# First token tile in two halves, the second tile ahead of the last first weights, and six warm-up products in place of nine

## The chip, the core and the metric

The kernel runs on one core of a Trainium2 chip. The core has a matrix engine (PE, with its weight loads shown apart as PEld), a vector engine (DVE), a scalar engine (ACT), GpSimd (POOL) and a queue processor (SP) that issues most transfers. PE multiplies a stationary block of 128 x 128 with a moving block of up to 512 columns and adds into one of eight banks of PSUM. The metric is the device time in microseconds of one execution; lower is better.

## The reference

One residual block over 512 tokens of width 1024 in float32: an input projection of the normalised tokens feeds a pooling mixer and a gated recurrence (a causal convolution, gates and a scan over the tokens), both merged by gates; then a gated feed-forward part with a convolution, and a gated embedding.

```python
h = rms_norm(x, g_mix_pre[l])
z = h @ w_in[l]                       # 1024 x 4608: pool 512, recurrence 1024, its gate 1024, gates 2048
u_pool, u_rx, u_rg = z[..., :c0], z[..., c0:c1], z[..., c1:c2]
y_pool = pool_mixer(u_pool, pool_w[l], pool_scale[l]) @ w_pool_out[l]
y_rnn = rg_lru_branch(u_rx, u_rg, ...) @ w_rg_out[l]
x = x + rms_norm((gate_pool * y_pool + gate_rnn * y_rnn) @ w_o[l], g_mix_post[l])
...                                   # feed-forward: w_up, causal convolution, gelu, w_down
x = x + ple_gate * ple
```

The part that matters here is the very first: the first 512 columns of `u_rx`, the projection that the recurrence needs first.

## The kernel before

Products are made in float32 precision from parts: each operand is a high part (a cast, on ACT) and a low part (value minus high part, on DVE), and a product is high x high + low x high + high x low. `quad("A")` holds the tokens' high and low parts (tiles A in the profile); `hi` and `lo` are those of a weight block, `raw` the block as fetched.

Tokens come transposed: `x_t[k]` is tile k, 128 channels by all 512 tokens, fetched into `xraw[k]` (tiles m in the profile). There are eight. For each, ACT multiplies by the norm's gain `gmix` into the high part (L556) and DVE makes the low part (L557). `gmix` is a small transfer of its own on ACT's queue (L229). The row scale of the norm is applied later, to the results.

The weights for the first four output tiles, `w_rx`, come in four blocks of two channel tiles each (`("rx", 0)` to `("rx", 3)`). The first block is fetched and cast in three pieces, columns 0 to 256, 256 to 512 and 512 to 1024 (`FIRST`, L464 to 474); the first two serve channel tile 0, the third serves tile 1. The stage's products (L580 to 586) go over the eight channel tiles; for each, 4 output tiles x 3 parts, 512 columns each, into four banks: 96 products.

Before that, `WARM` products of a 128 x 128 block of ones run on PE (L240, L241; in float32 each shows as two passes). Nothing reads their result.

After the 96 products come the tiles of the rest of `w_in` (`in_tile`, L641). Inside the first of them, after three channel tiles, `spread_rstd` (L633 to 638) runs four small products of `ones` with four diagonals (tiles t in the profile), which spread the tokens' row scales over all partitions. DVE makes the diagonals at L591 from the scales.

PE's order is that of the code. On the other engines a scheduler orders the instructions from the order of the code, their dependencies and a few explicit ones (`behind`). SP issues its transfers in order, and each waits for the landing of the eighth one before it among these queues. The line that makes the diagonals:

```python
behind(V.tensor_scalar(diag[:, t * P : (t + 1) * P], ident, rstd1[:, t : t + 1], None, ALU.mult), low_of["in", 0])
```

Of the kernel before, what the change touches and what calls it, by code (L numbers as in the profile page):

```python
# [53 lines left out]

PLACES, PLACE_UP, PLACE_H2 = 64, 48, (1072, 46)
URGENT = 700
WARM = 9

FIRST = (0, 256), (256, 512), (512, 1024)
IN_ORDER = [("gate", _g) for _g in range(4)]  # L60
# [23 lines left out]
def block_kernel(  # L84
# [361 lines left out]
    def prep(key):  # L446
        if key[0] == "up" and key not in parts:
            up_form(*key[1:])
            return
        if key in parts:  # L450
            hi, lo = parts_of(D)
            for i, v in enumerate((hi, lo)):
                nc.sync.dma_start(v.bitcast(F32), parts[key][i])
            if key[0] == "up":
                hi, lo = (v.rearrange("p (j c) -> p j c", j=2) for v in (hi, lo))
            ready[key] = (hi, lo)
            return
        ap = src[key]
        n = 1
        for d in ap.shape[1:]:  # L460
            n *= d
        raw = wpool.tile([P, n], F32, tag="raw", name=nm("raw"), bufs=6)
        dst = raw if len(ap.shape) == 2 else raw.rearrange("p (k c) -> p k c", k=ap.shape[1])
        if key == order[0]:  # L464
            nc.sync.dma_start(xraw[0], x_t[0])
            for a, b in FIRST:
                nc.sync.dma_start(raw[:, a:b], ap.rearrange("p k c -> p (k c)")[:, a:b])
        else:
            nc.sync.dma_start(dst, ap)
        hi, lo = parts_of(n)  # L470
        if key == order[0]:
            for a, b in FIRST:
                ACT.copy(hi[:, a:b], raw[:, a:b])
                sub(lo[:, a:b], raw[:, a:b], hi[:, a:b].bitcast(F32))
        else:
            ins = ACT.copy(hi, raw)  # L476
# [68 lines left out]
        )  # L545
        xtok.append(xt)

    for k in range(KD):
        raw = xraw[k]
        if k == 0:  # L550
            weight(("rx", 0), ahead=0)
        else:
            nc.sync.dma_start(raw, x_t[k])
        hi, lo = ht(k)
        g = gmix[:, k : k + 1]
        ht_done.append(ACT.activation(hi, raw, AF.Identity, scale=g).ins.name)  # L556
        V.scalar_tensor_tensor(lo, raw, g, hi.bitcast(F32), ALU.mult, ALU.subtract)  # L557
        if k == 3:
# [21 lines left out]
    for k in range(KD):  # L580
        w = weight(("rx", k // 2), ahead=3)
        (wh, wl), (hh, hl) = w, ht(k)
        for i, (a, b) in enumerate(((wh, hh), (wl, hh), (wh, hl))):
            for m in range(4):
                o = (k % 2) * S + m * P
                PE.matmul(rx[m], a[:, o : o + P], turns(b), start=k == 0 and i == 0, stop=k == KD - 1 and i == 2)  # L586


    diag = temp()
# [939 lines left out]
```

## Time and profile before

| what | us |
|---|---|
| runs | 703.17, 703.72, 703.90 |
| median | 703.72 |
| the profiled execution | 702.84 |
| its span, first to last instruction | 701.1 |

The profile is of one execution. It has the busy time of each engine, the chain of work that ended last, groups of like instructions, the timeline of each engine and the transfers with the time from issue to landing. Times count from the span's start. PE's lengths overlap, since one product starts before the last has ended; how often they start is read from the start times, or from a group of n as (length of the group - length of one) / (n - 1). DVE is busy for 591.6 us of the span, ACT for 454.2, and the 16 DMA engines move 251 GB/s on the mean.

### The profile page before, as it was taken

The page shows a single profiled execution, that of the slowest core. Times are in us where ns is not written, and L with a number is a line of the kernel's source. Part 1 is how long each engine was busy: PE and PEld are TensorE (multiplying, and loading weights), DVE is VectorE, ACT ScalarE, POOL GpSimd, SP SyncE. Part 2 cuts the span into 40 slices and gives each one's busy share as a digit, 9 for nine tenths or more (in the row PEclk, how much of TensorE's full clock was granted, in tenths as well). Part 3 has the DMA queues.
Part 4 walks back from the last instruction along what each step waited for, and adds up shares of the span by engine and source line. Part 5 has one row for each costly group of instructions (what it writes and reads, how often), then busy time and mean ns, then how long its engine had stood idle before and what let it go on. Part 6 is the DMA issues. An engine that isn't in the chain of part 4 may idle for free.

```text
span 701.1 us, 11599 instructions
## 1 busy us (share of the span) xinstructions
PE 693.4 (99%) x4423; PEld 638.2 (91%) x4423; DVE 591.6 (84%) x772; ACT 454.2 (65%) x693; POOL 97.5 (14%) x123
## 2 busy tenths in 40 slices
PE   9999999999999999999999999999999999999997
PEld 8888888888889998889999999999999888888886
DVE  5698645999759998897999999999999988989972
ACT  6757789934438574488966667766667747665631
POOL 0311331322000000112011211111210210001100
PEclk9999999999999999999999999999999999999999
DMA  8999899999898897865396886896699799967111
GB/s 323 410 304 282 237 245 225 258 264 290 252 334 286 302 385 251 326 214 180 118 328 206 196 264 211 206 261 238 169 219 386 238 300 328 346 207 260 56 61 61
DMA packets 67288, 175.71 MB, mean 251 GB/s; under 512 B 6049, under 2 KB 6689, under 8 KB 66849
## 3 DMA queue, kind: packets, MB, share of 16 engines
q1 hardware_dynamic: 49808, 124.64, 49.3%
q0 software_dynamic: 17280, 50.34, 30.6%
q8 instruction: 35, 0.57, 0.3%
q14 instruction: 21, 0.16, 0.1%
q10 hardware_dynamic: 144, 0.00, 0.0%
HBM read 162.37 MB, written 62.91 MB: 321 GB/s over the span
## 4 chain that ended last, share of the span: by engine, by line
PE 89%; DVE 5%; ACT 1%; issue 1%; POOL 1%; DMA 1%; SPq 0%; ACTq 0%; DVEq 0%; POOLq 0%
PE ps L222 28%; PE ps L224 28%; PE ps L223 28%; PE ps L586 3%; POOL s L507 1%; DVE lo L191 1%; PE ps L695 1%; DMA raw<-in_w_rx_dram 1%; DVE C L191 1%; DVE m L1017 1%; PE ps L1028 0%; DMA x2d<-m 0%; DVE m L1091 0%; DVE m L1222 0%; ACT rb L512 0%
## 5 line engine op out<-in xcount | busy, mean ns | idle before, releaser
L191 DVE TENSOR_TENSOR lo<-raw,hi 128x1024 fp32r<-128x1024 f32 (+2 forms) x199 | 230.3, 1183 | 47.0 <-ACT hi L476 30.3
L222 PE MATMUL ps<-A,hi 128*128 128x256 f32 (+1 forms) x672 | 212.0, 316 | 0.5 <-ACT ps L1216 0.5
L224 PE MATMUL ps<-A,lo 128*128 128x256 f32 (+1 forms) x672 | 211.4, 315 | 0.0
L223 PE MATMUL ps<-A,hi 128*128 128x256 f32 (+1 forms) x672 | 211.4, 315 | 0.0
L476 ACT CAST hi<-raw 128x1024 fp32r<-128x1024 f32 (+1 forms) x118 | 118.2, 1013 | 58.8 <-PE ps L224 19.5
L222 PEld LDWEIGHTS ps<-A,hi 128*128 128x128 f32 x672 | 128.2, 191 | 8.8 <-issue 1.0
L224 PEld LDWEIGHTS ps<-A,lo 128*128 128x128 f32 x672 | 128.3, 191 | 6.9
L223 PEld LDWEIGHTS ps<-A,hi 128*128 128x128 f32 x672 | 128.2, 191 | 6.7
L224 PE MATMUL ps<-C,lo 128*128 128x256 f32 x376 | 103.3, 275 | 1.3 <-DVE lo L191 1.3
L222 PE MATMUL ps<-C,hi 128*128 128x256 f32 x376 | 103.7, 276 | 0.1
L223 PE MATMUL ps<-C,hi 128*128 128x256 f32 x376 | 103.3, 275 | 0.0
L195 ACT CAST hi<-raw 128x1024 fp32r<-128x1024 f32 x76 | 78.6, 1051 | 20.2 <-PE ps L223 13.1
L222 PE MATMUL ps<-hi,A 128*128 128x512 f32 x224 | 85.2, 380 | 0.0
L224 PE MATMUL ps<-hi,A 128*128 128x512 f32 x224 | 85.0, 379 | 0.0
L223 PE MATMUL ps<-lo,A 128*128 128x512 f32 x224 | 84.9, 379 | 0.0
L224 PEld LDWEIGHTS ps<-C,lo 128*128 128x128 f32 x376 | 71.8, 191 | 1.5 <-DVE lo L191 1.5
L222 PEld LDWEIGHTS ps<-C,hi 128*128 128x128 f32 x376 | 71.8, 191 | 0.6 <-ACT ps L1161 0.4
L223 PEld LDWEIGHTS ps<-C,hi 128*128 128x128 f32 x376 | 71.8, 191 | 0.3
L507 POOL TENSOR_TENSOR s<-s,mhalf 128x1 f32<-128x1 f32 (+1 forms) x21 | 17.6, 840 | 265.6 <-DVE s L523 243.8
L307 POOL DMA_DIRECT2D wdsum<-in_w_down_dram x36 | 33.2, 1056 | 141.2 <-ACT t L1157 63.5
L224 PEld LDWEIGHTS ps<-hi,A 128*128 128x128 f32 x224 | 42.3, 189 | 6.3 <-DVE A L191 0.4
L222 PEld LDWEIGHTS ps<-hi,A 128*128 128x128 f32 x224 | 42.3, 189 | 6.0
(206 smaller groups left out, 1070.9 us busy)
## 6 DMA issues: line engine op xcount, KB each, us to landing
raw<-in_w_up_dram SPq DMA_DIRECT2D x46, 512.0 KB, 5.4
wdsum<-in_w_down_dram POOLq DMA_DIRECT2D x36, 512.0 KB, 7.7
raw<-in_w_in_dram SPq DMA_DIRECT2D x32, 512.0 KB, 8.7
raw<-wdsum SPq DMA_DIRECT2D x24, 512.0 KB, 7.8
raw<-in_w_down_dram SPq DMA_DIRECT2D x18, 512.0 KB, 6.9
wosum<-in_w_o_dram POOLq DMA_DIRECT2D x12, 512.0 KB, 9.4
wdsum<-wdsum POOLq DMA_DIRECT2D x12, 512.0 KB, 5.9
raw<-wosum SPq DMA_DIRECT2D x8, 512.0 KB, 6.2
```

The lines of the kernel that those rows point to most:

```text
L191: return V.tensor_tensor(o, a, b, ALU.subtract)
L195: last_copy[0] = ACT.copy(hi, src)
L222: PE.matmul(o, ah, bh, start=start, stop=False, **kw)
L223: PE.matmul(o, ah, bl, start=False, stop=False, **kw)
L224: PE.matmul(o, al, bh, start=False, stop=stop, **kw)
L307: ins = nc.gpsimd.dma_start(o, i, **kw)
L476: ins = ACT.copy(hi, raw)
L507: last_pow[0] = nc.gpsimd.tensor_tensor(y, v, mhalf[:, :n], ALU.pow).ins.name
L586: PE.matmul(rx[m], a[:, o : o + P], turns(b), start=k == 0 and i == 0, stop=k == KD - 1 and i == 2)
L695: PE.matmul(ps, bd[pr, a, o], turns(b[pr]), start=i == 0, stop=i == 2)
L1017: ins = V.scalar_tensor_tensor(res[h], og[h], r, res[h], ALU.mult, ALU.add)
```

## The change

Three edits, all at the start.

The first token tile is fetched in two halves. A half (`quarters_of`) is two stretches of 128 tokens, 256 apart, since the products read the tokens in an interleaved order. Transfers, high parts and low parts of the halves alternate with the first two weight pieces. The second token tile is fetched and split ahead of the third weight piece. The products of channel tile 0 are made in the order of arrival: for two output tiles and half the tokens at a time, 256 columns each, 24 products in place of 12. The six of one such part need only one weight piece and one half of the tokens. `WARM` is 6.

```diff
-WARM = 9
+WARM = 6
...
         if key == order[0]:
-            nc.sync.dma_start(xraw[0], x_t[0])
-            for a, b in FIRST:
+            for j, (a, b) in enumerate(FIRST):
+                if j < 2:
+                    nc.sync.dma_start(quarters_of(xraw[0], j), quarters_of(x_t[0], j))
+                else:
+                    nc.sync.dma_start(xraw[1], x_t[1])
                 nc.sync.dma_start(raw[:, a:b], ap.rearrange("p k c -> p (k c)")[:, a:b])
...
         if key == order[0]:
-            for a, b in FIRST:
+            for j, (a, b) in enumerate(FIRST):
+                first_tokens(j)
                 ACT.copy(hi[:, a:b], raw[:, a:b])
                 sub(lo[:, a:b], raw[:, a:b], hi[:, a:b].bitcast(F32))
...
+    def quarters_of(v, j):
+        return v.rearrange("p (a b) -> p a b", a=2)[:, :, j * P : (j + 1) * P]
+
+    def tokens(k, j=None):
+        hi, lo, raw = (v if j is None else quarters_of(v, j) for v in (*ht(k), xraw[k]))
         g = gmix[:, k : k + 1]
         ht_done.append(ACT.activation(hi, raw, AF.Identity, scale=g).ins.name)
         V.scalar_tensor_tensor(lo, raw, g, hi.bitcast(F32), ALU.mult, ALU.subtract)
+
+    def first_tokens(n):
+        if n < 2:
+            tokens(0, n)
+        else:
+            tokens(1)
...
         (wh, wl), (hh, hl) = w, ht(k)
+        for q, h in ((0, 0), (0, 1), (1, 0), (1, 1)) if k == 0 else ():
+            for i, (a, b) in enumerate(((wh, hh), (wh, hl), (wl, hh))):
+                for m in (2 * q, 2 * q + 1):
+                    PE.matmul(rx[m][:, h * HALF : (h + 1) * HALF], a[:, m * P : (m + 1) * P], turns(b)[:, h * P : (h + 1) * P, :], start=(h, i) == (0, 0), stop=i == 2, skip_group_check=True)
+        if k == 0:
+            continue
         for i, (a, b) in enumerate(((wh, hh), (wl, hh), (wh, hl))):
             for m in range(4):
                 o = (k % 2) * S + m * P
-                PE.matmul(rx[m], a[:, o : o + P], turns(b), start=k == 0 and i == 0, stop=k == KD - 1 and i == 2)
+                PE.matmul(rx[m], a[:, o : o + P], turns(b), start=False, stop=i == 2, skip_group_check=True)
```

Where the instructions stand. On SP, from the program's start, before (m is a token tile, raw a weight block):

```order
L465 DMA m_139<-in_x_t_dram 128x512
L467 DMA raw_147<-in_w_rx_dram 128x256 x2
L467 DMA raw_147<-in_w_rx_dram 128x512
L553 DMA m_140<-in_x_t_dram 128x512
L469 DMA raw_165<-in_w_rx_dram 128x1024
```

and after:

```order
L467 DMA m_136<-in_x_t_dram 128x2x128
L470 DMA raw_144<-in_w_rx_dram 128x256
L467 DMA m_136<-in_x_t_dram 128x2x128
L470 DMA raw_144<-in_w_rx_dram 128x256
L469 DMA m_137<-in_x_t_dram 128x512
L470 DMA raw_144<-in_w_rx_dram 128x512
L472 DMA raw_165<-in_w_rx_dram 128x1024
```

One transfer more stands ahead of the second weight block, and the second token tile has gone ahead of the third weight piece. On ACT, the same place, before:

```order
L556 ACTIVATE A_135<-m_139,gmix 128x512
L473 CAST hi_152<-raw_147 128x256 x2
L473 CAST hi_152<-raw_147 128x512
L556 ACTIVATE A_135<-m_140,gmix 128x512
L476 CAST hi_167<-raw_165 128x1024
```

and after:

```order
L558 ACTIVATE A_132<-m_136,gmix 128x2x128
L477 CAST hi_151<-raw_144 128x256
L558 ACTIVATE A_132<-m_136,gmix 128x2x128
L477 CAST hi_151<-raw_144 128x256
L558 ACTIVATE A_132<-m_137,gmix 128x512
L477 CAST hi_151<-raw_144 128x512
L480 CAST hi_167<-raw_165 128x1024
```

The two halves alternate with the weight pieces, and the second tile's tokens precede the third piece. DVE's low parts stand in the same order. On PE, after the warm-up products, the first six products after the change (ps_263 and ps_264 are the banks of the first two output tiles, A_132 and A_134 the high and low tokens):

```order
L602 MATMUL ps_263<-A_132,hi_151 128x256
L602 MATMUL ps_264<-A_132,hi_151 128x256
L602 MATMUL ps_263<-A_134,hi_151 128x256
L602 MATMUL ps_264<-A_134,hi_151 128x256
L602 MATMUL ps_263<-A_132,lo_152 128x256
L602 MATMUL ps_264<-A_132,lo_152 128x256
```

Before, these were products of 512 columns over all four banks, with the low weights ahead of the low tokens. From the second channel tile on, PE, ACT, DVE, POOL and SP issue the same instructions in the same order before and after.

More of the change, by code (lines that the diff above doesn't have):

```diff
@@ L546, in load_tokens @@
         xtok.append(xt)
[L548 to L554, printed above, removed]
+    def quarters_of(v, j):
+        return v.rearrange("p (a b) -> p a b", a=2)[:, :, j * P : (j + 1) * P]
+    def tokens(k, j=None):
+        hi, lo, raw = (v if j is None else quarters_of(v, j) for v in (*ht(k), xraw[k]))
         g = gmix[:, k : k + 1]
@@ L557, in block_kernel @@
         V.scalar_tensor_tensor(lo, raw, g, hi.bitcast(F32), ALU.mult, ALU.subtract)
+    def first_tokens(n):
[3 more added lines that the diff above has]
+            tokens(1)
+    for k in range(KD):
+        if k == 0:
+            weight(("rx", 0), ahead=0)
+            ht_done.pop(0)
+        elif k > 1:
+            nc.sync.dma_start(xraw[k], x_t[k])
+            tokens(k)
         if k == 3:
```

1 line of the change is left out of this document (added).

## The prediction

> **What bounds the kernel now.** I read the busy times first, then the chain that ended last, then each engine's timeline of the first 30 us, since everything the change touches lies there.
>
> ```profile
> PE 693.4 (99%) x4423; PEld 638.2 (91%) x4423; DVE 591.6 (84%) x772; ACT 454.2 (65%) x693; POOL 97.5 (14%) x123
> ...
> 1.66 3.77 DMA raw<-in_w_rx_dram
> ...
> 5.90 20.56 PE ps L586 x94
> ...
> 349.63 0.11 PE ps L223
> ```
>
> PE is busy for 693.4 of 701.1 us. The chain (start, duration, what) begins with a fetch of the first weights and then stays on the 94 first products, L586. A microsecond won on PE at the start reaches the end only if no other engine holds PE up later. The last row prices a product of 256 columns: 0.11 us. These are the first rows of PE, then ACT, DVE and SP (start, duration, line, out<-in, in brackets the idle time before and what ended it):
>
> ```profile
> 1.06 4.21 PE L241 MATMUL ps<-m 128*128 128x128 f32 x18 [1.06 <-DVE mhalf L235]
> 4.92 0.80 PE L586 MATMUL ps<-A,hi 128*128 128x512 f32 x2
> 5.90 0.70 PE L586 MATMUL ps<-A,hi 128*128 128x512 f32 x2 [0.17 <-ACT hi L473]
> 6.44 1.03 PE L586 MATMUL ps<-A,lo 128*128 128x512 f32 x4
> 7.30 1.89 PE L586 MATMUL ps<-A,hi 128*128 128x512 f32 x8
> ...
> 3.64 0.72 ACT L556 ACTIVATE A<-m,gmix 128x512 fp32r<-128x512 f32 x1 [0.97 <-DMA gmix<-in_cols_dram]
> 4.27 0.39 ACT L473 CAST hi<-raw 128x256 fp32r<-128x256 f32 x1
> 5.45 0.40 ACT L473 CAST hi<-raw 128x256 fp32r<-128x256 f32 x1 [0.79 <-DMA raw<-in_w_rx_dram]
> 6.28 0.62 ACT L473 CAST hi<-raw 128x512 fp32r<-128x512 f32 x1 [0.43 <-DMA raw<-in_w_rx_dram]
> 6.96 0.73 ACT L556 ACTIVATE A<-m,gmix 128x512 fp32r<-128x512 f32 x1
> 9.54 0.72 ACT L556 ACTIVATE A<-m,gmix 128x512 fp32r<-128x512 f32 x1
> ...
> 5.06 0.42 DVE L191 TENSOR_TENSOR lo<-raw,hi 128x256 fp32r<-128x256 f32 x1
> 6.93 0.69 DVE L191 TENSOR_TENSOR lo<-raw,hi 128x512 fp32r<-128x512 f32 x1 [0.62 <-ACT hi L473]
> 7.72 0.75 DVE L557 SCALAR_TENSOR_TENSOR A<-m,gmix,A 128x512 fp32r<-128x512 f32 x1
> ...
> 0.75 0.39 SPq L465 DMA_DIRECT2D m<-in_x_t_dram  x1
> 1.19 1.37 SPq L467 DMA_DIRECT2D raw<-in_w_rx_dram  x3
> 2.60 0.43 SPq L553 DMA_DIRECT2D m<-in_x_t_dram  x1
> 11.50 0.33 SPq L469 DMA_DIRECT2D raw<-in_w_in_dram  x1
> ```
>
> Nine warm-up products, two passes each, fill PE to 4.92. The eight products from 7.30 start (1.89 - 0.38) / 7 = 0.216 us apart, 0.38 being the length of the last; the two from 4.92 start 0.80 - 0.38 = 0.42 apart, so PE still ran at half speed there. (The granted-clock column reads 1.00 throughout; I go by spacing.) After two products PE has nothing to do until the second weight quarter is cast: 4.92 + 0.80 = 5.72 to 5.90. The second token tile's products start at 7.30 + 4 x 0.216 = 8.17.
>
> **The bound that decides.** At 28 us PE runs four small products (L637) that spread the row scales. Each needs a 128-column diagonal from DVE. Rows of ACT, DVE, PE and its weight loads:
>
> ```profile
> 23.42 1.04 ACT L476 CAST hi<-raw 128x1024 fp32r<-128x1024 f32 x1 [0.64 <-DMA raw<-in_w_in_dram]
> 24.69 1.04 ACT L476 CAST hi<-raw 128x1024 fp32r<-128x1024 f32 x1 [0.23 <-DMA raw<-in_w_in_dram]
> ...
> 24.49 2.50 DVE L191 TENSOR_TENSOR lo<-raw,hi 128x1024 fp32r<-128x1024 f32 x2 [1.51 <-ACT hi L476]
> 26.91 0.67 DVE L591 TENSOR_SCALAR t<-ident,s 128x128 f32<-128x128 f32 x3
> 27.50 1.22 DVE L191 TENSOR_TENSOR lo<-raw,hi 128x1024 fp32r<-128x1024 f32 x1
> 28.63 0.28 DVE L591 TENSOR_SCALAR t<-ident,s 128x128 f32<-128x128 f32 x1
> ...
> 28.24 0.83 PE L637 MATMUL ps<-t,m 128*128 128x128 f32 x6
> 28.97 0.30 PEld L637 LDWEIGHTS ps<-t,m 128*128 128x128 f32 x2
> 29.21 0.46 PE L222 MATMUL ps<-A,hi 128*128 128x512 f32 x1
> ```
>
> Six of the eight passes start (0.83 - 0.27) / 5 = 0.11 apart, the last at 28.79; the seventh is due at 28.90 and starts at 28.97, after the fourth diagonal (28.63 + 0.28 = 28.91). PE already waits 0.07 us here. That diagonal stands on DVE behind a train without a gap from 24.49 on, which began when ACT had cast the weights that landed at 23.4. It depends on when w_in lands, not on how far PE is.
>
> **What paces the landings.** Two views: the DMA issues (KB each, us from issue to landing) and the stretches (last two columns: DMA share, GB/s).
>
> ```profile
> gmix<-in_cols_dram ACTq DMA_DIRECT2D x1, 4.0 KB, 2.9
> m<-in_x_t_dram SPq DMA_DIRECT2D x1, 256.0 KB, 2.7
> raw<-in_w_rx_dram SPq DMA_DIRECT2D x1, 128.0 KB, 3.8
> m<-in_x_t_dram SPq DMA_DIRECT2D x1, 256.0 KB, 4.3
> raw<-in_w_in_dram SPq DMA_DIRECT2D x1, 512.0 KB, 11.9
> ...
> 3.00:4.00 1.00, 1.00 (x7) 1.00 (x6) 0.00 (x0) 0.36 (x1) 0.00 (x0) 1.00 0.80 150
> 4.00:5.00 1.00, 1.00 (x7) 1.00 (x6) 0.61 (x1) 0.65 (x2) 0.00 (x0) 1.00 0.71 187
> 5.00:6.00 1.00, 0.83 (x5) 0.42 (x3) 0.60 (x3) 0.40 (x1) 0.00 (x0) 1.00 0.99 380
> 10.00:15.00 5.00, 5.00 (x25) 4.38 (x24) 4.64 (x6) 4.04 (x6) 0.00 (x0) 1.00 1.03 410
> ```
>
> From 5 us on the queues are full at 380 to 410 GB/s; the w_in tile issued at 11.50 lands 11.9 later. Its landing moves only by what the first 5 us deliver, and the change sends the same bytes.
>
> **The change, step by step.** SP issues one transfer more: tokens a, weights a, tokens b, weights b, tile 1, weights c. At 0.43 us an issue (row at 2.60) everything behind leaves up to 0.43 later. I cost this at nothing, because the queue hides it: tile 1, issued at 2.60, took 4.3 us to land at 6.9. If that cover is missing, w_in is late by up to 0.43. At their places in the bytes, weights b should land as now (1.66 + 3.77 = 5.43 in the chain), tile 1 where weights c land now (6.28 at the latest), and weights c where tile 1 lands now, 6.9.
>
> ACT: its first operation waits for gmix (0.74 + 2.9 = 3.64), not for the tokens (0.75 + 2.7 = 3.45). Half the columns cost about the 0.39 of the 256-column cast, so hi of tokens a is ready at 4.03, of weights a at 4.42. [...]
>
> Warm-ups: 18 passes start (4.21 - 0.42) / 17 = 0.22 apart, so 12 end at 1.06 + 11 x 0.22 + 0.42 = 3.9. PE idles for about 0.5 us and starts at 4.45, not 4.92: 0.47 earlier. Bounds: 3.9 if gmix comes sooner in a lighter queue, 4.92 if the first cast is no earlier.
>
> PE's first tile: 24 products of 0.11 = 2.64 us where 12 x 0.216 = 2.59 stood, 0.05 more. The twelve of weights a take 4.45 to about 6.2, the first four at half speed (0.213 each, to 5.3), with DVE's low parts (0.42 to 0.43 each, back to back from 4.05) in time for them. Weights b are cast at 5.45 + 0.40 = 5.85, so the 0.18 us hole goes. The other twelve end at 6.2 + 12 x 0.11 = 7.5.
>
> Tile 1: ACT from 6.28 to 7.0, then the cast of weights c, 0.62, ready at 7.6. PE starts tile 1 there instead of at 8.17: 0.55 earlier. DVE does 0.75 + 0.69 from 7.0 to 8.45, due at 7.6 + 0.86. Tile 2 would follow at 7.6 + 12 x 0.216 = 10.2, but its tokens are ready at 9.54 + 0.72 = 10.26. Now it starts at 8.17 + 12 x 0.216 = 10.76, so the lead is 10.76 - 10.3 = 0.46.
>
> The small products: PE arrives at 28.24 - 0.46 = 27.78, does six passes by 28.4, and waits for the fourth diagonal until 28.97, as now. L222 follows at 29.21, as now. The whole lead of 0.46 becomes a wait of 0.5. After that both programs issue the same instructions in the same order on every engine.
>
> Sum: 0.46 won, 0.46 waited, 0.0 on the span of 701.1. The profiled execution took 702.84 with 1.74 around the span; the median of the runs shown is 703.72, 0.88 above. On the runs I predict 703.7. Within 0.2% (1.4 us) is what a measurement of this kernel cannot tell from no change.
>
> **Rivals.**
> - *The lead is kept.* From 3 to 5 us only 150 and 187 GB/s moved, (2 x 390 - 337) / 390 = 1.1 us of full rate lost. If other shapes at the start remove part of that dip, rx and w_in land sooner, the diagonals with them, and PE keeps its lead. Against it: the queue was not empty in the dip and no row says what ended it. Worth 0.2 to 0.95 (PE's first tile ends at 7.5, or at 7.2 if it can start at 3.9, against 8.17 now): 702.8 to 703.5, say 703.1. It alone does not reach 0.2%.
> - *The landings slip.* The extra issue and smaller pieces (512 bytes a row) delay w_in by 0.2 to 0.6: about 704.1.
> - *Slower, because PE's clock comes late.* Now PE works without a break from 1.06 and reaches full speed after the slow pair, between 5.34 and 6.44. The change leaves a hole between 3.9 and 4.45. If the count begins anew there, 5.34 - 1.06 = 4.3 us of work from 4.45 end at 8.75: 20 slow half products by then, four fast, tile 1 at 9.2 instead of 8.17, 1.03 - 0.07 = 0.95 slower, 704.6. It decides (over 1.4 slower) if full speed comes after about 10 us: 24 x 0.213 = 5.1 puts tile 1 at 9.6, which is already 1.4 late. Against it: unbroken work is all that the trace shows before full speed, so no row tells what a hole does. [...]
>
> **Numbers.** No change, the lead lost at the diagonals: 0.42 (703.3 to 704.1 by itself). Lead kept: 0.24, of it 0.09 beyond 0.2% if small waits fall well besides. Landings slip: 0.10, of it 0.02 beyond. Clock late: 0.24, of it 0.15 beyond, since a count that a hole breaks may also begin later than at 4.45. Faster 0.09, same 0.74, slower 0.17. Range 702.7 to 705.1: down to the kept lead, up to the point from which the clock decides.
>
> **What would show it.** Right: PE's first half product near 4.45, tile 1 near 7.6, a new wait of about 0.5 before the last two passes of the small products, L222 near 29.2, w_in's first cast at 23.4. Wrong: that cast moved by more than 0.3 (either landing rival), or products of 256 columns 0.21 apart past 6 us (the clock). A change behind 30 us would mean that I missed a coupling.

## The result, and the profile after

The changed kernel took 704.51 us (median of 14 runs, 703.51 to 709.36), the kernel before 702.99 beside it; the ratio is 1.0024, 95% interval 1.0013 to 1.0035. A second comparison gave 1.0028 [1.0015, 1.0041]. It is slower by about 1.7 us. The forecast was no change. The profiled execution took 707.39 (span 705.5), 2.9 above the median of its kernel, so its waits are larger than those of most executions; a second profiled one took 707.39 as well.

SP's first issues after the change (start, duration, line, out<-in):

```profile
0.75 0.67 SPq L467 DMA_DIRECT2D m<-in_x_t_dram  x1
1.47 0.58 SPq L470 DMA_DIRECT2D raw<-in_w_rx_dram  x1
2.10 0.57 SPq L467 DMA_DIRECT2D m<-in_x_t_dram  x1
2.71 0.59 SPq L470 DMA_DIRECT2D raw<-in_w_rx_dram  x1
3.35 0.43 SPq L469 DMA_DIRECT2D m<-in_x_t_dram  x1
3.82 0.43 SPq L470 DMA_DIRECT2D raw<-in_w_rx_dram  x1
4.30 0.43 SPq L472 DMA_DIRECT2D raw<-in_w_rx_dram  x1
```

The two half fetches take 0.67 and 0.57 us to issue, and the weight pieces behind them 0.58 and 0.59, where an issue took 0.39 to 0.46 before. The second weight block leaves at 4.30, before at 3.07. The stretches of one microsecond (last two columns: DMA share, GB/s) show that the queue did not hide this. Before, the first of them (the next one stands in the prediction):

```profile
2.00:3.00 1.00, 1.00 (x7) 1.00 (x6) 0.00 (x0) 0.65 (x2) 0.00 (x0) 1.00 0.96 330
```

and after:

```profile
2.00:3.00 1.00, 1.00 (x7) 1.00 (x6) 0.00 (x0) 0.63 (x2) 0.00 (x0) 1.00 0.57 171
3.00:4.00 1.00, 0.99 (x5) 0.69 (x4) 0.07 (x1) 0.51 (x1) 0.00 (x0) 1.00 0.65 189
```

The DMA engines were busy for 57% and 65% of these two stretches, before for 96% and 80%: the transfers waited for their issue. PE and ACT after, and from the chain of waits the second weight block's fetch:

```profile
4.46 1.22 PE L602 MATMUL ps<-A,hi 128*128 128x256 f32 x4 [0.47 <-ACT hi L477]
5.90 1.06 PE L602 MATMUL ps<-A,hi 128*128 128x256 f32 x4
7.12 0.61 PE L602 MATMUL ps<-A,hi 128*128 128x256 f32 x4
8.46 1.03 PE L608 MATMUL ps<-A,hi 128*128 128x512 f32 x4
11.83 1.13 PE L608 MATMUL ps<-A,hi 128*128 128x512 f32 x4 [0.61 <-ACT A L558]
29.42 1.05 PE L659 MATMUL ps<-t,m 128*128 128x128 f32 x8
30.23 0.46 PE L222 MATMUL ps<-A,hi 128*128 128x512 f32 x1
...
6.21 0.72 ACT L558 ACTIVATE A<-m,gmix 128x512 fp32r<-128x512 f32 x1 [0.39 <-DMA m<-in_x_t_dram]
10.11 1.05 ACT L480 CAST hi<-raw 128x1024 fp32r<-128x1024 f32 x1 [2.40 <-DMA raw<-in_w_rx_dram]
24.58 2.93 ACT L480 CAST hi<-raw 128x1024 fp32r<-128x1024 f32 x3
...
4.30 5.79 DMA raw<-in_w_rx_dram
```

The second weight block lands at 10.1 instead of 8.57; ACT casts it ahead of the third tile's tokens, so PE idles 0.61 us and starts that tile at 11.83 (before 10.76). The first tile's products of 256 columns start (1.06 - 0.42) / 3 = 0.21 apart at 5.90 and 0.11 apart at 7.12: full speed came at about 7. PE reaches the small products at 29.42, 1.2 later than before, and no longer waits there; L222 follows at 30.23 instead of 29.21.

So 1.0 us is gone by 30 us in this execution. The rest goes later. Here is how much later than in the profile of before the same product starts (products counted from the end, where the order is the same in all kernels; the column heads are the start before):

| profiled execution | at 90 us | 197 | 232 | 311 | last | 
|---|---|---|---|---|---|
| changed | 1.02 | 1.02 | 3.13 | 4.51 | 4.47 |
| changed, second profile | 1.49 | 1.49 | 2.65 | 4.11 | 4.57 |

Nothing happens between 30 and 197 us, then three waits come. PE's waits from 200 to 300 us after (us in total, times, longest; the same view of before is empty), rows of ACT and POOL behind them, and the stores among the DMA issues (last number: us from issue to landing):

```profile
PE ps L224 <- DVE A L191: 1.1, 1, 1.1
PE ps L222 <- ACT hi L480: 0.7, 1, 0.7
PE ps L224 <- DVE lo L191: 0.6, 1, 0.6
...
191.58 1.05 ACT L480 CAST hi<-raw 128x1024 fp32r<-128x1024 f32 x1 [5.68 <-DMA parts<-hi]
...
181.02 1.05 POOL L307 DMA_DIRECT2D up2sum<-in_w_up_dram  x1 [4.02 <-DMA up2sum<-up2sum]
...
parts<-hi SPq DMA_DIRECT2D x2, 512.0 KB, 8.0
```

The rows of ACT, POOL and the stores before:

```profile
188.97 1.04 ACT L476 CAST hi<-raw 128x1024 fp32r<-128x1024 f32 x1 [4.09 <-issue]
...
177.25 1.05 POOL L307 DMA_DIRECT2D up2sum<-in_w_up_dram  x1 [1.78 <-DMA up2sum<-up2sum]
...
parts<-hi SPq DMA_DIRECT2D x2, 512.0 KB, 6.4
```

From 183 us on, split weights are stored to memory (`parts`), and ACT reuses the tiles when a store has landed. POOL's chain of weight sums in memory (`sum_in_dram`, each step waiting for the landing of an earlier one) ends at about that time: its last sum is issued 3.8 us later than before, the stores take 8.0 us instead of 6.4, and ACT's cast comes 2.6 us later. That train of store, cast and fetch runs from 186 to 226 us and hands its lateness to PE at 211, 225 and 275. This is read from one profile; the runs without the last two sums test it.

### The profile page after: what moved, and what is told of

Same layout as the page of the kernel before. It is cut to its first block, busy times and chain, and to the rows that moved or that the text cites. A ratio compares the mean times of both kernels' runs of the same rounds, so it can differ in the third digit from the quotient of the medians.

```text
span 705.5 us, 11615 instructions
## 1 busy us (share of the span) xinstructions
PE 694.5 (98%) x4429; PEld 638.5 (91%) x4429; DVE 592.0 (84%) x773; ACT 454.3 (64%) x694; POOL 97.0 (14%) x123
## 4 chain that ended last, share of the span: by engine, by line
PE 64%; DVE 15%; DMA 10%; ACT 7%; issue 3%; POOL 1%; SPq 1%; ACTq 0%; DVEq 0%; POOLq 0%
PE ps L222 20%; PE ps L224 20%; PE ps L223 20%; DMA parts<-hi 3%; DVE lo L191 3%; PE ps L608 2%; ACT m L166 2%; DVE m L746 1%; DMA lo<-parts 1%; ACT hi L480 1%; ACT t L166 1%; ACT hi L195 1%; POOL s L511 1%; DMA m<-in_x_dram 1%; DMA raw<-rg0sum 1%
## 5 line engine op out<-in xcount | busy, mean ns | idle before, releaser
L222 PE MATMUL ps<-A,hi 128*128 128x256 f32 (+1 forms) x672 | 212.1, 316 | 0.5 <-ACT ps L1238 0.5
L222 PEld LDWEIGHTS ps<-A,hi 128*128 128x128 f32 x672 | 128.2, 191 | 8.9 <-issue 1.0
L222 PE MATMUL ps<-C,hi 128*128 128x256 f32 x376 | 103.7, 276 | 0.1
L222 PE MATMUL ps<-hi,A 128*128 128x512 f32 x224 | 85.2, 380 | 0.0
L222 PEld LDWEIGHTS ps<-C,hi 128*128 128x128 f32 x376 | 71.8, 191 | 0.6 <-ACT ps L1183 0.3
L224 PEld LDWEIGHTS ps<-hi,A 128*128 128x128 f32 x224 | 42.3, 189 | 7.5 <-DVE A L191 1.5
L223 PEld LDWEIGHTS ps<-lo,A 128*128 128x128 f32 x224 | 42.4, 189 | 5.9
```

The costliest lines, as they stand in the source:

```text
L222: PE.matmul(o, ah, bh, start=start, stop=False, **kw)
L223: PE.matmul(o, ah, bl, start=False, stop=False, **kw)
L224: PE.matmul(o, al, bh, start=False, stop=stop, **kw)
```

## The experiments

Each kernel was compared with the kernel before on the same chip. The first four were written for two theories: A, late issues on SP; B, the late clock. Later, P is A narrowed to the pieces of 512 bytes, C is one transfer more however it is cut, and S is POOL's sums.

| run | ratio to before | medians apart, us | at 90 us | 197 | 232 | 311 | last |
|---|---|---|---|---|---|---|---|
| nine warm-ups | 1.0022 [1.0009, 1.0036] | 1.61 | 0.66 | 0.66 | 1.22 | 0.99 | 1.26 |
| six warm-ups alone | 1.0005 [0.9994, 1.0017] | 1.02 | -0.20 | -0.20 | -0.20 | -0.43 | 0.87 |
| split fetch alone | 1.0016 [1.0004, 1.0027] | 1.57 | 3.36 | 3.36 | 4.20 | 4.20 | 5.17 |
| whole fetch | 1.0005 [0.9991, 1.0018] | 0.57 | 1.72 | 1.72 | 1.72 | 1.64 | 1.87 |
| rows of 1024 bytes | 1.0002 [0.9986, 1.0018] | 1.01 | 0.32 | 0.32 | 0.32 | 0.09 | 0.18 |
| the same again | 1.0007 [0.9996, 1.0018] | 0.29 | 0.40 | 0.40 | 0.42 | 0.19 | 0.28 |
| one more issue | 0.9994 [0.9979, 1.0008] | -0.64 | -0.21 | -0.21 | -0.21 | -0.42 | -0.14 |
| pieces alone | 1.0009 [0.9992, 1.0025] | 0.16 | 2.43 | 2.44 | 2.44 | 2.21 | 2.37 |
| whole fetch, nine | 1.0008 [0.9993, 1.0022] | 0.53 | 0.94 | 0.94 | 1.59 | 2.66 | 3.31 |
| second tile ahead alone | 1.0007 [0.9998, 1.0015] | 0.65 | 0.60 | 0.60 | 1.41 | 1.18 | 1.21 |
| diagonals in one row | 1.0039 [1.0026, 1.0052] | 3.12 | -0.04 | -0.04 | 3.82 | 3.60 | 3.73 |
| changed, fewer sums | 0.9999 [0.9982, 1.0016] | 0.94 | 0.80 | 0.80 | 0.80 | 0.57 | 0.79 |
| before, more sums | 1.0003 [0.9984, 1.0022] | 0.21 | 0.62 | 0.62 | 0.62 | 0.40 | 1.21 |
| diagonals, fewer sums | 0.9983 [0.9966, 0.9999] | -0.51 | 0.14 | 0.15 | 0.15 | -0.08 | 0.12 |
| before, fewer sums | 0.9981 [0.9964, 0.9998] | -0.68 | 0.05 | 0.05 | 0.05 | -0.18 | -0.01 |
| before, sums later | 1.0034 [1.0021, 1.0047] | 2.49 | 0.72 | 0.72 | 0.72 | 3.12 | 3.21 |
| diagonals, sums later | 1.0028 [1.0016, 1.0040] | 2.07 | 0.24 | 0.24 | 0.24 | 2.70 | 2.86 |

The lateness columns are of one profiled execution each, as above; the ratio and the medians are of all runs. The two do not always say the same: the medians lie up to 1.02 us apart where the interval of the ratio still holds 1, and such a difference is neither shown nor excluded.

**Nine warm-ups in the changed kernel.**

```diff
-WARM = 6
+WARM = 9
```

> The changed kernel with nine warm-up products again, all else of the change kept. Theory A (issue): SP spends 0.57 to 0.67 us on each of the four small transfers, the second weight block leaves at 4.30 instead of 3.07 and lands at 10.1, and tile 2's products start at 11.8 instead of 10.8; warm-ups don't touch that, so tile 2 starts within 0.2 of 11.8 and the time stays about 1.5 us over the kernel before (ratio about 1.002). Theory B (clock): the hole in PE from 3.9 to 4.46 put off full speed from 5.2 to 7.05; without the hole full speed comes by 5.5 and about 1 us comes back (ratio 1.000 to 1.001).

The loss stays, 1.0022. In the profile full speed came at 4.2 us (the 18 warm-up passes took 3.75 us, before 4.21), tile 1's products had no late clock ahead of them, and the second weight block still left at 4.31. It landed at 9.2 and the third tile started at 10.9, not at 10.1 and 11.8 as A had it, so in this execution the late issue cost less. The hole after six warm-ups is not what makes the change slow.

**Six warm-ups alone, in the kernel before.**

```diff
-WARM = 9
+WARM = 6
```

> The kernel before with six warm-up products, nothing else changed. Theory A (issue): no change, ratio 0.9995 to 1.0005; tile 2 is at most 0.3 us later than 10.76, since the second weight block lands at 8.6 as before. Theory B (clock): the hole before the first product puts off full speed to 7 or later; the first tile's twelve products take 1 us longer, tile 2 starts at 11.3 or later, ratio about 1.001 to 1.002.

1.0005, by its interval not told from no change. The medians lie 1.02 us apart (0.41 to 1.37 by drawing the runs anew), so a cost of the missing warm-ups is not excluded. The profile shows none at the start: PE idled from 4.0 to 4.7 and again before 5.9, and the two products at 4.73 ran at full speed all the same (0.70 us together, like the two at 5.86). This hole did not put the clock off.

**The split fetch alone, in the kernel before.**

```diff
-            nc.sync.dma_start(xraw[0], x_t[0])
-            for a, b in FIRST:
+            for j, (a, b) in enumerate(FIRST):
+                if j < 2:
+                    halves = [v.rearrange("p (a b) -> p a b", a=2)[:, :, j * P : (j + 1) * P] for v in (xraw[0], x_t[0])]
+                    nc.sync.dma_start(*halves)
```

> The kernel before with only the first tile's fetch split in two halves of 512-byte pieces, alternating with the weight pieces; products whole, nine warm-ups, second tile's fetch behind the third weight piece as before. Theory A (issue): the second weight block leaves SP at 4.0 or later and lands at 9.5 or later, tile 2 starts at 11.3 or later, about 1 us slower than before (ratio about 1.0015). Theory B (clock): PE has no hole, so no change of the time (ratio within 0.0005 of 1).

1.0016. The issues are as slow as in the changed kernel (0.68, 0.58 and 0.56 us), and the second weight block leaves at 4.32. The scheduler also put a weight cast ahead of the first tokens on ACT, so the run holds a little more than the fetch.

**The whole fetch in the changed kernel.**

```diff
-                if j < 2:
-                    nc.sync.dma_start(quarters_of(xraw[0], j), quarters_of(x_t[0], j))
-                else:
-                    nc.sync.dma_start(xraw[1], x_t[1])
+                if j != 1:
+                    nc.sync.dma_start(xraw[j // 2], x_t[j // 2])
```

> The changed kernel with the first tile fetched in one transfer again; its parts, its products in halves, the second tile ahead of the third weight piece and six warm-ups stay. Theory A (issue): SP's issues go back to 0.4 us, the second weight block leaves at about 3.1 and lands at 8.6, tile 2 starts at 10.3 to 10.8, and the time is that of the kernel before or up to 0.4 less (ratio 0.9995 to 1.000). Theory B (clock): the hole stays (its first product is ready at about 4.7), full speed comes at 7 or later, and the time stays about 1 us over the kernel before (ratio 1.001 to 1.002).

1.0005, though the profiled execution had the late clock as the prediction's rival described it:

```profile
5.06 1.22 PE L600 MATMUL ps<-A,hi 128*128 128x256 f32 x4 [1.07 <-ACT hi L475]
8.64 0.63 PE L600 MATMUL ps<-A,lo 128*128 128x256 f32 x2
9.83 0.39 PE L600 MATMUL ps<-A,lo 128*128 128x256 f32 x2
10.05 1.03 PE L606 MATMUL ps<-A,hi 128*128 128x512 f32 x4
```

A hole of 1.07 us, products at half speed until 9.7, the second tile at 10.05; this execution ends 1.9 us later. Of the eleven executions four lie at 703.0 to 703.3 and five at 704.4 or more, the profiled 704.72 among them, so some may pay that and some not; only the profiled one shows its clock. A is borne out by the ratio, and B is not excluded as a cost in some executions.

**Rows of 1024 bytes.** The host lays the first tile half after half, so that a half is one run of 1024 bytes a row.

```diff
-                    nc.sync.dma_start(quarters_of(xraw[0], j), quarters_of(x_t[0], j))
+                    nc.sync.dma_start(xraw[0][:, j * HALF : (j + 1) * HALF], x_t[0][:, j * HALF : (j + 1) * HALF])
```

> The changed kernel, with the first token tile laid half after half in memory, so that each half is one run of 1024 bytes a row in place of two runs of 512. Seven issues on SP up to the second weight block as in the changed kernel, same bytes, same order. Theory P (the pieces of 512 bytes make the issues slow, and the slow issues make everything behind late): each early issue takes 0.39 to 0.45 us instead of 0.57 to 0.67, the second weight block leaves at 3.4 to 3.6 instead of 4.30 and lands by 9.3, the second token tile's products start at 10.3 to 11.0, the ratio to the kernel before is 0.999 to 1.001. Theory C (one transfer more is what costs, however it is cut): the ratio stays at 1.002 and PE waits 0.5 us or more at 224 to 227 us. With six warm-ups the clock may still come late: full speed at 5 to 7 us.

SP's issues in this run:

```profile
0.75 0.38 SPq L467 DMA_DIRECT2D m<-in_x_t_dram  x1
1.19 0.42 SPq L470 DMA_DIRECT2D raw<-in_w_rx_dram  x1
1.66 0.42 SPq L467 DMA_DIRECT2D m<-in_x_t_dram  x1
3.55 0.43 SPq L472 DMA_DIRECT2D raw<-in_w_rx_dram  x1
```

The same seven transfers with the same bytes: the issues are as short as before, and the second weight block leaves at 3.55, 0.48 later than before. From 2 to 4 us the DMA engines are busy for 82% and 94% of the time. The ratio falls to 1.0002, though the medians are still 1.01 us apart. At the small products PE waits as the prediction drew it:

```profile
28.21 0.83 PE L661 MATMUL ps<-t,m 128*128 128x128 f32 x6
29.29 0.49 PE L661 MATMUL ps<-t,m 128*128 128x128 f32 x2 [0.25 <-DVE t L615]
```

Six passes, then a wait for the fourth diagonal: the seventh was due at 28.87 (28.21 + 6 x 0.11) and starts at 29.29, 0.42 later. But PE comes there at 28.21, only 0.03 earlier than before; it waits because the diagonal is ready at 29.23 (before 28.91).

The edit changes two things at once: a row is one run and not two, and the runs are longer than 512 bytes. No run here separates them.

**One more issue in the kernel before.**

```diff
+        if k == 1:
+            nc.sync.dma_start(spare, cols[:, C_GMIX : C_GMIX + KD])
```

> The kernel before, with one more transfer on SP's queue behind the second token tile: 4 KB of the small columns into a tile that nothing reads. Nothing else moves. This is the step that I had costed at nothing with a bound of 0.43 us, alone. Theory P: the issue costs 0.43, the second weight block leaves at 3.5 instead of 3.07; PE's second token tile at 10.7 to 11.2; ratio 0.9995 to 1.0007, no wait of 0.4 us or more at 224 to 227. Theory C: ratio 1.001 to 1.003, and the wait at 224 to 227 appears.

The second weight block leaves at 3.55, as with rows of 1024 bytes, and the kernel is not slower (0.9994). C falls: one issue of 0.43 us costs nothing here, as I had said.

**The pieces alone, in the kernel before.** The first tile's rows lie in four pieces of 512 bytes with 16 bytes between them; one transfer.

```diff
-            nc.sync.dma_start(xraw[0], x_t[0])
+            nc.sync.dma_start(*(v.rearrange("p (a c) -> p a c", a=4)[:, :, :P] for v in (xraw[0], x_t[0])))
```

> The kernel before, with the first token tile fetched in one transfer as before, but from rows that lie in four pieces of 512 bytes with 16 bytes between them. Number and order of transfers as before. Theory P: this issue takes 0.6 to 1.4 us in place of 0.39, those behind it are slower too (0.55 or more in place of 0.42), the second weight block leaves 0.8 to 1.5 later than 3.07, and the ratio is 1.0005 to 1.002. Theory C: 0.999 to 1.0005, no matter how slow the issues are.

```profile
0.75 0.67 SPq L465 DMA_DIRECT2D m<-in_x_t_dram  x1
1.47 1.55 SPq L467 DMA_DIRECT2D raw<-in_w_rx_dram  x3
3.54 0.43 SPq L469 DMA_DIRECT2D raw<-in_w_rx_dram  x1
```

The issue itself is slow (0.67), but the three behind it take 1.55 together, hardly more than 1.37 before, and the second weight block is only 0.47 late. The ratio, 1.0009, is not told from none. P had expected 0.8 to 1.5: one such transfer is not shown to be a loss. The split fetch, which has two of them with other issues between, showed one.

**The whole fetch with nine warm-ups.** On top of the edit of the whole fetch:

```diff
-WARM = 6
+WARM = 9
```

> The changed kernel with the first token tile fetched in one transfer and with nine warm-ups: left of the change are the products by halves and the second token tile ahead of the last first weights. If the hole after six warm-ups was what put PE's full speed off to 9.72 in the run with the whole fetch and six, full speed comes at 4 to 5.5 here, the second token tile's products at 10.3 to 10.9 instead of 12.64, and the ratio falls from 1.0005 to 0.999 to 1.0000. If the rest of the start carries the loss there, the ratio stays at 1.0005 or above. Theory P has no loss here (no pieces of 512 bytes).

1.0008. Full speed came at 7.0 us even with nine warm-ups and no hole, where 4 to 5.5 was expected, so the run gives no price of the hole. The profile has the waits at 225 and 275 as well: they are not the split fetch's alone.

**The changed kernel and the rows of 1024 bytes again, side by side.**

> The changed kernel as it is, beside the runs that follow. The lost time at the start should come again: the second weight block issued at 4.3 and landed past 9, PE at L222 0.7 to 1.3 us later than 29.21, ratio 1.0015 to 1.003. The waits of 0.9 to 1.4 us near 211, 225 and 275 us decide between two readings: if the change brings them, two or three of them come again; if they are chance landings in a stretch that hangs on stores and fetches (190 to 225 us), this profile shows others, or at most one.

> The changed kernel with the first tile's halves as single rows of 1024 bytes, a second time, on the same chip as the changed kernel. Theory P (the 512-byte pieces of the two half fetches make the early issues slow, that is most of the loss): 0.9995 to 1.0008, and below the changed kernel by 0.1% or more. Theory C (something else in the change): no difference to the changed kernel.

1.0028 and 1.0007. The medians differ by 1.34 us; drawing the runs anew gives 0.62 to 2.72. In this comparison, side by side, that one edit of the layout takes back most of the loss. Waits of PE near 211, 225 and 275 us came again in the changed kernel (by the start times 0.6, 0.6 and 1.2 us lost), and not with the rows of 1024 bytes. In this profile full speed came at 9.9 us and tile 1 at 9.76, where the other one had 7.0 and 8.46. Its second weight block left at 4.31 and yet landed at 8.66, hardly later than before. So the same kernel lost 1.5 us at the start to the clock in one execution, and in the other 1.0 us, where the landing at 10.1 held PE up.

Over all profiles, the block landed at 8.66 to 11.14 in the five where it left at 4.3, and at 8.44 to 9.44 in the five whose first transfers are those of before. That the layout carries the loss is shown; that it does so through this landing in every execution is not.

**The second tile ahead, alone, in the kernel before.**

```diff
+                if j == 2:
+                    nc.sync.dma_start(xraw[1], x_t[1])
```

> The kernel before, with one part of the change alone: the second token tile is fetched and split ahead of the last first weights. Whole first tile, whole products, nine warm-ups. Predicted for this part: the last weights land at 6.9 in place of 6.3 and are cast at about 7.6, PE's products with them wait or not by that; the second tile's products start no later than 10.8. Theory P: 0.9995 to 1.0005. If this part carries a loss of its own, 1.0008 or more, with PE waiting 0.3 us or more between 6 and 9 us for weights c.

1.0007 [0.9998, 1.0015]: at most a small loss. The cast of weights c stood at 7.54 and PE waited 0.95 us for the second weight piece, cast at 6.21. That piece left at 1.66 as before and landed at 6.19; whether the transfer moved up behind it did that is not shown. With the first transfers of before it landed at 5.4 to 5.9.

**The diagonals in one row.** Rows of 1024 bytes, and DVE makes all four diagonals behind the first low parts.

```diff
-    for t in range(NT):
-        behind(V.tensor_scalar(diag[:, t * P : (t + 1) * P], ident, rstd1[:, t : t + 1], None, ALU.mult), low_of["in", 0])
+    with tc.high_priority(offset=URGENT):
+        for t in range(NT):
+            behind(V.tensor_scalar(diag[:, t * P : (t + 1) * P], ident, rstd1[:, t : t + 1], None, ALU.mult), low_of["in", 0])
```

> The changed kernel with rows of 1024 bytes as above, and the four diagonals for the small products in one row on DVE behind the low parts of the first input weights, instead of three, then other low parts, then the fourth. In the profile with rows of 1024 bytes PE waited 0.52 us for the fourth diagonal at 28.76. If that diagonal is what takes PE's lead, as predicted, the wait falls below 0.1, L222 starts at 28.9 to 29.1 instead of 29.53, and the time is 0.3 to 0.5 us lower than with the rows of 1024 bytes alone: 0.9990 to 1.0003. If another wait follows within the first 40 us, as long as the first, the time does not move.

The small products no longer wait (eight passes from 28.36) and L222 starts at 29.17 instead of 29.53: the diagonal was the bound at 29 us. The expected time was missed: with five executions, the kernel is the slowest of all, 1.0039. The lateness is -0.04 us until 197 and 3.82 at 232:

```profile
191.87 1.04 ACT L480 CAST hi<-raw 128x1024 fp32r<-128x1024 f32 x1 [7.00 <-DMA parts<-hi]
...
211.97 0.48 PE L222 MATMUL ps<-m,hi 128*128 128x512 f32 x1 [1.61 <-ACT hi L480]
...
181.56 1.05 POOL L307 DMA_DIRECT2D up2sum<-in_w_up_dram  x1 [2.23 <-DMA up2sum<-up2sum]
...
parts<-hi SPq DMA_DIRECT2D x2, 512.0 KB, 9.4
...
210.00:214.00 4.00, 2.37 (x9) 1.44 (x8) 2.64 (x4) 2.01 (x5) 0.00 (x0) 0.95 0.93 335
214.00:217.00 3.00, 3.00 (x8) 2.37 (x8) 1.92 (x3) 2.10 (x4) 0.00 (x0) 0.50 0.89 271
```

The last sum late, the stores at 9.4 us, ACT 7.0 us idle, PE 1.6; and then (third column from the right) the granted clock is 0.50 for a stretch of 3.4 us, half of it, 1.7 us, lost once more.

**Without the last two sums.** The same edit in the changed kernel, in the variant with the diagonals and in the kernel before:

```diff
-    sum_in_dram(chain_of(sums_of("rg"), sums_of("wo"), sums_of("up")), None)
+    sum_in_dram(chain_of(sums_of("rg"), sums_of("wo"), sums_of("up")), 46)
```

> The changed kernel without the last two of POOL's weight sums in memory (the second addends of the last sums for up tiles 1 and 2 are left out, so those products lack a term; everything else is computed). Theory S: POOL's chain of sums ends later in the changed kernel (its last sum is issued at 181 to 182 us, at 177.3 before), runs into the stores of the split output weights at 183 to 188, these land late (8 us instead of 6.4), ACT waits for them to free its tiles (5.6 to 6.0 us near 186 instead of 4.1), and that train reaches PE at 211, 225 and 275. Without the last two sums: the stores land within 6.5 us, ACT's wait near 186 is at most 4.5, no wait of PE of 0.5 or more at 205 to 280, and the ratio falls from 1.0024 to 1.0028 to about 1.0010 to 1.0017, what the late start alone costs. If the sums are not it: 1.002 or above and the waits stay.

> Rows of 1024 bytes with the four diagonals in one row, which was 1.0039, without the last two sums (left out as above). Theory S: its loss was the sums' (last one issued at 181.6, ACT waited 7.0 us at 185, PE 2.0 us at 210, after which the clock was halved for 3.4 us): without them 0.9985 to 1.0003. If not: 1.002 or above.

> The kernel before without the last two sums (left out as above), the base for the two runs that leave them out. Theory S: the stores are free of them, but PE had no wait there in the profile of before: 0.9990 to 1.0000. If leaving them out is worth 0.1% or more here too, that much has to be taken off the others.

Changed kernel without the last two sums, ACT and the stores (as above):

```profile
188.28 1.04 ACT L480 CAST hi<-raw 128x1024 fp32r<-128x1024 f32 x1 [2.60 <-DMA parts<-hi]
...
parts<-hi SPq DMA_DIRECT2D x2, 512.0 KB, 4.9
```

ACT waits 2.6 us instead of 5.7, the stores take 4.9, and PE has no wait from 200 to 300 in any of the three kernels without these sums. With the diagonals the ratio goes from 1.0039 to 0.9983 (on two chips): the 3 us were the sums'. The kernel before gains too, more than I had expected (0.9981): it suggests that its own executions meet the train at times, though the profiled one did not. Against that base the changed kernel still loses: 704.62 against 703.00, 1.62 us (0.97 to 1.92 by drawing the runs anew). That is as much as the 1.52 and 1.63 between the two complete kernels, so what they differ by in a usual execution is the start; the sums add up to 3 us more in the profiled ones. The variant with rows of 1024 bytes and the diagonals, without the sums, stands at 703.17 on the same chip, 1.45 below the changed kernel (0.73 to 1.85). The diagonals' part of that, by the start of L222, is about 0.36; the rest points to the layout once more.

**Two more copies, in the kernel before.** They go to memory that nothing reads, ahead of the last two sums.

```diff
-    sum_in_dram(chain_of(sums_of("rg"), sums_of("wo"), sums_of("up")), None)
+    sums = list(chain_of(sums_of("rg"), sums_of("wo"), sums_of("up")))
+    more = [(dram.tile([P, 2, S], F32, name=f"more{f}"), up_block(1, f), {}) for f in (11, 12)]
+    sum_in_dram(sums[:46] + more + sums[46:], None)
```

> The kernel before, with two more copies of 512 KB within memory on POOL's queue, ahead of the last two sums; nothing reads them. Start unchanged. Theory S: the last sum lands 3 to 6 us later, into the stores at 183 to 188; ACT's wait there grows from 4.1 to 5.5 or more; PE waits 0.4 us or more at 211 or 225; ratio 1.001 to 1.004, though the first 150 us are as before. If the sums are not it: 0.999 to 1.0007.

A miss: 1.0003. In the profile the chain was early, its last sum left at 178.4 in spite of the copies, the stores took 6.3 us, ACT waited 4.0, and PE had no wait. In all profiles the waits go with how long before the first store the last sum leaves. In the 15 profiles of complete kernels with the sums in their place, it left 0.9 to 4.6 us before in seven, and PE lost 0.56 to 3.9 us between 197 and 232 in each of them; it left 4.8 to 8.1 us before in eight, and PE lost nothing there (at most 0.02). This run is one of the eight, at 4.8, so the copies were too few, and it counts neither for S nor against it; its outcome lies in the range that I had given for S being wrong.

**The last two sums later.** They wait until ACT has made its first copy of the products of the recurrence's output, at 226.8 us; in the kernel before and in the variant with the diagonals, both complete.

```diff
-    sum_in_dram(chain_of(sums_of("rg"), sums_of("wo"), sums_of("up")), None)
+    all_sums = chain_of(sums_of("rg"), sums_of("wo"), sums_of("up"))
+    sum_in_dram(all_sums, 46)
...
                 if f == 1:
-                    ACT.copy(ra[i][:, :HALF], z)
+                    copied = ACT.copy(ra[i][:, :HALF], z).ins.name
+                    if p == i == 0:
+                        sum_in_dram(all_sums, None, copied)
```

> The kernel before, complete, with POOL's last two sums put off until ACT has made its first copy of the rg products (226.8 us), past the stores at 183 to 212 and ahead of their first reader at about 291. Theory S: as without these sums, the stores land within 5 to 6 us and the train from 186 to 226 is free of them: 0.9980 to 0.9995, and the runs lie closer together (0.6 to 1.5 us instead of 3 and more). If the sums only move the crowding to 227 to 245: 0.9995 to 1.002, with PE waits of 0.4 us or more there or at 275.

> The variant with rows of 1024 bytes and the four diagonals in one row (1.0039 with the sums where they were, 0.9983 without the last two), complete, with the last two sums put off in the same way. Theory S: 0.9980 to 1.0000, PE's waits at 210 to 226 below 0.4, no drop of the clock. If it stays above 1.002, leaving the sums out had helped by their bytes and not by their place. Against the run of before with later sums it shows what the halves, the second tile ahead and the diagonals are worth together once the early issues are fast: by the profiles 0 to 0.3 us.

The stretch from 186 to 226 is clean in both (stores 4.9 to 5.0 us, no wait of PE), and both are slower, 1.0034 and 1.0028. PE's waits from 200 to 300 in the kernel before with later sums:

```profile
PE ps L222 <- ACT ps L986: 1.6, 1, 1.6
PE ps L224 <- DVE A L191: 0.6, 1, 0.6
```

The crowding moved to 240 us and handed itself on to 275, as the second reading in the expectation had it, though the ratio is above the 1.002 given for it. For the diagonals I had written that a time above 1.002 speaks for the sums' bytes and not for their place. The complete kernels without a wait (one more issue, both runs with rows of 1024 bytes) move the same bytes, so it is the place; 227 us is another bad one. By the medians two sums of 512 KB went with 2.07 to 3.12 us lost where they met a train that hangs on landings (the diagonals' variant, both kernels with later sums), and with -0.64 to 1.01 us in those three runs without a wait. No complete kernel here is shown to beat the kernel before.

## Why the prediction was wrong

- *The step that failed: "SP issues one transfer more. ... I cost this at nothing, because the queue hides it ... If that cover is missing, w_in is late by up to 0.43."* The count was right and harmless (one more issue: 0.9994). The price per issue was not: I took 0.43 from whole rows for transfers whose rows are cut into 512 bytes. Measured: 0.67 and 0.57 for them, 0.58 and 0.59 for the issues behind, the second weight block 1.23 us late at issue and 1.5 and 0.1 at landing in the two profiles. And the cover was not there: the 4.3 us that tile 1 took to land were read as a full queue, but with the DMA engines at 57 to 65% from 2 to 4 us the issue paced the start. With issues of 0.42 the same transfers came to 1.0002 and 1.0007, side by side 1.34 us less than the changed kernel. The rival "the landings slip" named the extra issue and the pieces, with a chance of 0.10, and put the time 0.4 above no change; measured were 1.5 and 1.6, and the runs bear out the pieces, not the extra issue.
- *PE's first product at 4.45:* it started at 4.46 (and 4.48), by luck. ACT began at 3.38 instead of 3.64 because gmix came sooner (0.74 + 1.7 = 2.44), and the half of the tokens took it 0.51 instead of 0.39. With rows of 1024 bytes the half tile landed at 2.99 instead of 3.44 and PE started at 4.05: the first step gained there.
- *Tile 1 at 7.6:* 8.46 and 9.76. The half products ran at half speed to 7.0 and 9.9, not 5.3. This is the rival of the late clock. Its price held in the second profile: full speed at 9.9, tile 1 at 9.76 for the 9.6 that it gave, 1.5 us lost for 1.4. Its condition did not: a count that the hole breaks would not give full speed at 4.7, 4.7 and 5.4 in other kernels with six warm-ups (holes of 0.7, 0.1 and 0.4), nor 7.0 with nine and no hole. The time of full speed differs between profiles of one kernel (7.0 and 9.9) and more between kernels (4.2 in the changed kernel with nine warm-ups, 10.4 with the pieces alone); no run shows what sets it. That the hole was not the cause of the change's loss the run with nine warm-ups shows; that a late clock adds to it in some executions stays possible.
- *The lead is lost at the fourth diagonal, a new wait of 0.5, L222 at 29.2:* not seen in the changed kernel, which arrives 1.2 late instead of early. With rows of 1024 bytes the bound is there: a wait of 0.42 and L222 at 29.53; with the diagonals in one row the wait is gone and L222 stands at 29.17. But the lead is not: PE arrives 0.03 us earlier and 0.42 later than before, not 0.46 earlier. Even with short issues the pieces landed later than I had placed them, weights b at 5.89 and 5.59 (5.43), tile 1 at 6.67 and 7.13 (6.28), weights c at 7.34 and 7.79 (6.9), so tile 1's products started at 8.03 and 8.48 instead of 7.6. There was no lead to lose.
- *w_in's first cast at 23.4:* 24.58, where ACT still had the tokens' squares to do, which came from a transfer issued 1.5 us later. It was one of the signs that I had named for a wrong forecast. In the second profile, where the second weight block landed early, the cast stood at 23.45 as forecast, and the other sign showed, half speed past 6 us.
- *"A change behind 30 us would mean that I missed a coupling":* I missed it. "The same instructions in the same order" does not fix when transfers meet. POOL's sums and the stores share the 16 DMA engines (from 182 to 190 us POOL's queue had 49.6% of their time and the other 45.2%, before 13.2% and 84.6%), and the last sum leaves 0.9 to 8.1 us ahead of the first store.

What stays open: why the chain of sums ends at 179 to 182 us in some kernels (changed, nine warm-ups, split fetch, both with the whole fetch, pieces, second tile ahead, diagonals) and at 174 to 177 in others. The lateness of the start alone is not it, since the variant with the diagonals had none. The first sums leave at 23 to 28 us, and the steps drift apart between 70 and 180. Nor is it settled why the profiled executions of the changed kernel met the train so much harder than its median, whether the length of the runs or their number makes an issue slow, and what six warm-ups cost by themselves.

## What to carry to other kernels

Price an issue by the shape of its rows (here 0.56 to 0.68 us for two runs of 512 bytes, 0.38 to 0.43 for one of 1024 or 2048), and ask whether the DMA engines are busy at that moment before calling it hidden; here a fetch cut into short runs was mended in the layout (1.0028 against 1.0007). Where one chain of transfers only has to be done some time and another hands buffers on by landings, look at when they meet: here a shift of 1 us far ahead (1.02 in the changed kernel), or none at all (-0.04 with the diagonals), stood ahead of 3.5 and 3.8 us lost from there on, and putting the slack chain elsewhere moved the cost to the next train here. Do not read a small gain off one early stage when such a train lies behind it.

## What the runs showed of the hardware that I had not expected

- Among the first issues on SP, one of 128 rows in two runs of 512 bytes takes 0.56 to 0.68 us (in four runs 0.67), in one run of 1024 or 2048 bytes 0.38 to 0.43. When issues with two runs stand between them, the plain issues take 0.58 to 0.60 instead of 0.42 to 0.46. Further back plain ones of 0.5 to 0.6 stand as well (0.58 at 8.06 us in the changed kernel).
- Full speed of PE came with six warm-ups at 4.7 us in the kernel before and at 9.9 in the second profile of the changed one, with nine at 4.2 in the changed kernel and at 10.4 with the pieces alone. Nine without a hole had it at 5.3 in the kernel before, at 4.2, and at 7.0 with the whole fetch. What makes the difference no run here shows.
- One wait of 1.61 us in the middle of the kernel, in the diagonals' variant, was followed by 3.4 us at a granted clock of 0.50; one of 1.56 in the kernel before with later sums was not (from 232 to 311 us that kernel fell back by 2.40 us, and its two waits alone are 2.2).
